# Nine rows in partitions 0-63 and seven in 64-127 for the last head's store of a query-key product

## The chip, the core and the metric

The kernel runs on one core of one Trainium2 chip. The metric is device time in microseconds (us) for one execution; lower is better. Before the change it is 1062.44 us, the median of three runs (1062.24 to 1063.06). The core has five engines that run side by side: PE (TensorE, matmuls), DVE (VectorE), ACT (ScalarE), POOL (GpSimd) and SP (SyncE, which here issues DMAs). Sixteen DMA engines carry data between the chip's HBM and the on-chip memory SBUF, which has 128 partitions. Matmul results land in PSUM and are copied from there to SBUF.

## The reference

```python
def setup_inputs():
    batch, n_heads, seq, head_dim = 8, 12, 1024, 64
    ...
def reference(q, k):
    return np.einsum('bhid,bhjd->bhij', q, k).astype(np.float32)
```

For each of 8 x 12 = 96 heads, the 1024 x 64 matrix q times the transposed 1024 x 64 matrix k: a 1024 x 1024 float32 result, 4 MB for a head and 402.65 MB in all. The inputs are 50.33 MB.

## The kernel before

**Blocks.** The 96 heads go in blocks of 2, 2, 4, 8 and then five times 16 heads (`sizes`). A block's q and k are loaded, cast to float16 on POOL, and transposed so that the 64 elements of a row lie along partitions: by PE in the first two blocks, in 32x32 squares by DVE (L229) in the others. Two heads share the 128 partitions of a transposed tile: the first half of a block's heads in partitions 0-63, the second in 64-127. So the last head of all is in partitions 64-127 of its block's `qT` and `kT`.

**One head** is the work of `scores`. Its 1024 rows are dealt over 128 partitions, eight rows each: row i of the head is on partition i // 8, as its row t = i % 8. For each t, one weight load of 64x128 (L308: every eighth column of `qT`) and two matmuls of 512 columns (L311) fill 128x1024 of PSUM. From the second head on two values of t go together (`w` = 2): four matmuls fill half of PSUM, 128x2048 float32, and one ACT copy (L288) takes it to the output buffer. PSUM has two such regions (`halves_ps`), so PE fills one while ACT empties the other. A head takes four copies.

**Output.** Each head has one of three output buffers `o_sb` of 128 x 8 x 1024 float32, taken in turn (`outs`). When the last of the four copies is done, SP issues one DMA for the whole head (L301): partition p sends its eight rows, 32 KB, to 32 KB of HBM in one piece. The first copy of a head waits until the store that left from the same buffer, three heads ago, has landed (`out_free`, counted by `store_landing`, 16 for each DMA). All 96 stores are on SP's queue, in the order of the heads. At the very end SP waits for all three counts.

**Input buffer.** `x_sb` holds the raw rows of the coming block (q, then k). `input_busy` is the last cast that reads it. After the casts of the last block nothing reads or writes it.

**The helper `multiply`** gives the matmul's tile size as (64, 128) at L320: 64 rows of weights, 128 columns.

Of the kernel before, what the change touches and what calls it, by code (L numbers as in the profile page):

```python
# [8 lines left out]
P = 128  # L9
# [50 lines left out]
def kernel(  # L60
# [6 lines left out]
    nc = tc.nc  # L67

    B, H, S, D = q.shape
    NT = S // P  # L70
# [4 lines left out]
    of = out.rearrange("b h i j -> (b h) i j")  # L75
# [13 lines left out]
    x_sb = pool.tile([P, NMAX * S * D // P], F32, name="x_sb", tag="x")  # L89
# [10 lines left out]
    pe = Engine(nc, nc.tensor, "pe_done")  # L100
    act = Engine(nc, nc.scalar, "act_done")
    dve = Engine(nc, nc.vector, "dve_done")
    gps = Engine(nc, nc.gpsimd, "pool_done")
    sp = Engine(nc, nc.sync, "sp_done")
# [18 lines left out]
    n, at = S * D // P * 2, 8 * S // 2  # L123
# [8 lines left out]
    input_busy = []  # L132
    outs = Ring(o_sb)
    input_landing = [Landing(nc, f"x{i}_in") for i in range(2)]
    store_landing = {id(t): Landing(nc, f"out{i}_out") for i, t in enumerate(o_sb)}

    class Block:
# [117 lines left out]
        def scores(self, n, side, regions, w):  # L255
            half, g = divmod(n, self.N // 2)
            cs = slice(half * D, (half + 1) * D)
            qT = self.qk[0].rearrange("c (g m t) -> c g t m", t=NT, m=P)
            kT = self.qk[1].rearrange("c (g j) -> c g j", j=S)
            buf, out_free, out_busy = outs.next()  # L260
            written = {}
            for u in range(NT // w):
                ps, ps_free, ps_busy = regions.next()
                first = True
                for tt in range(w):
                    stationary = qT[cs, g, w * u + tt]
                    done = pe.run(
                        lambda: load_weights(stationary, half * D),
                        self.ready if n == 0 and u == 0 else [],
                        signal=False,  # L270
                    )
                    for j in range(2):
                        at = tt * S + j * 512
                        done = pe.run(
                            lambda: multiply(
                                ps[:, at : at + 512],
                                stationary,
                                kT[cs, g, j * 512 : (j + 1) * 512],
                                half * D,
                            ),  # L280
                            ps_free,
                            signal=tt == w - 1 and j == 1,
                        )
                dst = buf[:, w * u : w * u + w].rearrange("p t j -> p (t j)")
                by_dve = w == 1 and u % 2
                copier = dve if by_dve else act
                copied = copier.run(
                    lambda: (nc.vector.tensor_copy if by_dve else nc.scalar.copy)(  # L288
                        out=dst, in_=ps[:, : w * S]
                    ),  # L290
                    out_free + [done],
                )
                written[copier] = copied
                ps_busy.append(copied)
                for do in side.get(u, []):
                    do()
            self.over = [done]
            sp.wait(written.values())
            if self.first + n == 0:
                sp.wait(blocks[EARLY].landed[0])  # L300
            dma = nc.sync.dma_start(  # L301
                out=of[self.first + n].rearrange("(p t) j -> p (t j)", p=P),
                in_=buf.rearrange("p t j -> p (t j)"),
            )
            out_busy.append(store_landing[id(buf)].start(dma))

    def load_weights(stationary, at):
        return nc.tensor.ldweights(stationary, tile_position=(at, 0))  # L308

    def multiply(dst, stationary, moving, at):  # L310
        return nc.tensor.add_instruction(  # L311
            mybir.InstMatmult(
                name=nc.get_next_instruction_name(),
                ins=[nc.tensor.lower_ap(moving), nc.tensor.lower_ap(stationary)],
                outs=[nc.tensor.lower_ap(dst)],
                start_tensor_calc=True,
                stop_tensor_calc=True,
                ldweights=False,
                tile_position=(at, 0),
                tile_size=(D, P),  # L320
            )
        )

    blocks, first = [], 0
# [4 lines left out]
    early, _, early_busy = outs.next()  # L329
    raw = early.rearrange("p t j -> p (t j)")  # L330
    at = 0
# [17 lines left out]
    def next_load(eng):  # L349
        if stream:  # L350
            b, x = stream.pop(0)
            earlier = (b.i, 0) if x else (b.i - 1, 1)
            assert b.i == EARLY or not any((i, c[0]) == earlier for i, c in casts)
            b.load(x, eng)

    for x in range(2):
# [7 lines left out]
                out=ident,  # L364
                in_=ident,
# [9 lines left out]
    def to_half(last):  # L375
        while casts:
            i, c = casts[0]
            if i > last or (blocks[i], c[0]) in stream:
                return
            if not (rooms if i == PE_BLOCKS else halves).free():  # L380
                return
            done = blocks[i].cast_quads(*c)
            if i == 2:
                early_busy[:] = [done]
            casts.pop(0)

    def transposed(b, s):
        b.transpose_quads(*s)
        to_half(b.i)

    def block(i, heads, regions, w):
        b = blocks[i]
        nxt = blocks[i + 1] if i + 1 < len(blocks) else None
        for n in heads:
            side = {}
            if nxt and nxt.by_pe:
                if n == 1:
                    side = {
                        u: [
                            lambda x=u // 2: nxt.transpose_rows(  # L400
                                x, regions.next(), dve, nc.vector.tensor_copy
                            )
                        ]
                        for u in (1, 3)
                    }
            elif nxt:
                parts = nxt.chunks()
                at = TURNS if i > EARLY else [m * b.N // len(parts) for m in range(len(parts))]
                some = [s for m, s in zip(at, parts) if m == n]
                side = {0: [lambda s=s: transposed(nxt, s) for s in some]}  # L410
            at = LOADS.get(i, {1: 1, 7: 1})
            if n in at:
                side[at[n]] = side.get(at[n], []) + [lambda: next_load(act)]
            b.scores(n, side, regions, w)
            to_half(i + 2 + (n == b.N - 1))

    for b in blocks[:PE_BLOCKS]:
# [6 lines left out]
    for x in range(2):  # L424
        blocks[0].transpose_rows(
            x, quarters.next(), (dve, act)[x], (nc.vector.tensor_copy, nc.scalar.copy)[x]
        )
        to_half(2)
    block(0, [0], quarters, 1)
    halves_ps = Ring([ps_all[:, 2 * S :], ps_all[:, : 2 * S]])  # L430
    halves_ps.busy = [quarters.busy[2] + quarters.busy[3], quarters.busy[0] + quarters.busy[1]]
    block(0, [1], halves_ps, 2)
    for i in range(1, len(blocks)):
        block(i, range(blocks[i].N), halves_ps, 2)
# [31 lines left out]
```

## Time and profile before

| | |
|---|---|
| time, median of 3 runs (range) | 1062.44 us (1062.24 to 1063.06) |
| time of the profiled execution | 1062.84 us |
| its span, from first to last instruction | 1061.0 us |
| PE busy | 700.2 us (66%) |
| ACT busy | 697.1 us (66%) |
| DVE busy | 431.0 us (41%) |
| POOL busy | 354.2 us (33%) |
| moved by DMA over the span | 453.21 MB, mean 427 GB/s |
| share of the chain that ended last: DMA, ACT, PE | 65%, 16%, 7% |
| one store: size, count, median from issue to landing | 4096 KB, 96, 21.8 us |
| ACT copy of 128x2048 (L288), mean | 1859 ns, 384 in the group |
| matmul of 512 columns (L311), mean | 617 ns, 1536 |

How to read it: the page shows one profiled execution. Its slices cut the span in 40 equal parts and give the busy share of each in tenths; the row for DMA is the mean over the 16 DMA engines. A DMA queue's packet is one piece of a transfer on one engine. The chain that ended last goes back from the last instruction, at each step to what released it. The windows view gives, for stretches of the span in us, each engine's busy time with its instruction count, the clock granted to TensorE, the share of the 16 DMA engines' time taken by the packets that start in the stretch, and GB/s. The granted clock is 1.00 in this kernel.

### The profile page before, as it was taken

To read this page: it belongs to the slowest core of one execution; us is meant where nothing else is said; L and a number is where in the kernel's file an instruction comes from. 1 tells how busy PE (TensorE), PEld (TensorE's weight loads), DVE (VectorE), ACT (ScalarE), POOL (GpSimd) and SP (SyncE) were. 2 spreads that over 40 slices of the span, in tenths; PEclk is the share of its full clock that TensorE was granted. 3 is DMA by queue.
4 is the path that set the end of the run, shared out by engine and by line. 5 is a ranking of instruction groups with operands and counts; after the bars stand their busy time and mean duration, and the time that the engine had idled before them with its cause. 6 is when DMAs were issued, how large, how long until landed. Compare 5 with 4: busy or idle time off the path is not lost.

```text
span 1061.0 us, 3307 instructions
## 1 busy us (share of the span) xinstructions
PE 700.2 (66%) x1568; PEld 127.3 (12%) x800; DVE 431.0 (41%) x55; ACT 697.1 (66%) x386; POOL 354.2 (33%) x206
## 2 busy tenths in 40 slices
PE   6876744957477748567765856775584777778770
PEld 1111100111011101011111101111110111111110
DVE  2995939029193009339003907600761920000000
ACT  4766655857477747567756756775675777777771
POOL 7927465056380028064006509100913700000000
DMA  9999999999999999999999999999999999999997
GB/s 376 434 435 435 434 434 434 416 421 432 431 434 434 435 429 428 426 435 432 432 422 434 435 427 433 433 434 423 433 429 432 435 434 431 434 434 431 432 431 322
DMA packets 17009, 453.21 MB, mean 427 GB/s; under 512 B 1888, under 2 KB 1888, under 8 KB 2912
## 3 DMA queue, kind: packets, MB, share of 16 engines
q1 hardware_dynamic: 14976, 410.00, 89.7%
q10 hardware_dynamic: 2016, 42.99, 9.8%
q8 instruction: 9, 0.15, 0.0%
q14 instruction: 8, 0.07, 0.0%
HBM read 50.33 MB, written 402.65 MB: 427 GB/s over the span
## 4 chain that ended last, share of the span: by engine, by line
DMA 65%; ACT 16%; PE 7%; DVE 5%; POOL 4%; issue 1%; ACTq 0%; SPq 0%
DMA out_dram<-o_sb 60%; ACT o_sb L288 16%; PE ps_all L311 7%; DVE kT L229 4%; POOL half L210 3%; DMA x_sb<-in_k_dram 2%; DMA x_sb<-in_q_dram 2%; DVE qT L229 1%; DMA o_sb<-in_q_dram 0%; PE ps_all L243 0%; POOL qT L181 0%; DVE kT L250 0%; ACT kT L250 0%; ACTq L36 0%; SPq L169 0%
## 5 line engine op out<-in xcount | busy, mean ns | idle before, releaser
L288 ACT COPY o_sb<-ps_all 128x2048 f32<-128x2048 f32 (+1 forms) x384 | 694.8, 1859 | 333.5 <-DMA out_dram<-o_sb 290.2
L311 PE MATMUL ps_all<-kT,qT 64*128 64x512 f16 x1536 | 696.1, 617 | 328.6 <-ACT o_sb L288 312.8
L210 POOL CAST half<-x_sb 32x2048 f16<-32x2048 f32 x176 | 332.3, 1888 | 482.1 <-DMA x_sb<-in_q_dram 302.2
L229 DVE STREAM_TRANSPOSE qT<-half 128x2048 f16<-128x2048 f16 x22 | 202.6, 9478 | 268.1 <-POOL half L210 268.1
L229 DVE STREAM_TRANSPOSE kT<-half 128x2048 f16<-128x2048 f16 x22 | 202.5, 9539 | 137.5 <-POOL half L210 137.5
L308 PEld LDWEIGHTS <-qT 64*128 64x128 f16 x768 | 124.2, 162 | 897.4 <-issue 878.0
L229 DVE STREAM_TRANSPOSE kT<-kT 128x1024 f16<-128x1024 f16 x2 | 9.4, 4870 | 0.0
L229 DVE STREAM_TRANSPOSE qT<-qT 128x1024 f16<-128x1024 f16 x2 | 9.2, 4780 | 0.0
L210 POOL CAST qT<-o_sb 32x1024 f16<-32x1024 f32 x8 | 8.3, 1035 | 1.2 <-DMA o_sb<-in_q_dram 0.8
L210 POOL CAST kT<-o_sb 32x1024 f16<-32x1024 f32 x8 | 8.3, 1035 | 0.5
L250 DVE COPY qT<-ps_all 128x1024 f16<-128x1024 f16 x2 | 2.4, 1224 | 11.1 <-PE ps_all L243 11.1
L288 DVE COPY o_sb<-ps_all 128x1024 f32<-128x1024 f32 x4 | 4.9, 1225 | 4.4 <-PE ps_all L311 4.4
L243 PE MATMUL ps_all<-ident,qT 128*128 128x128 f16 x16 | 2.1, 311 | 6.8 <-POOL qT L181 6.7
L250 ACT COPY kT<-ps_all 128x1024 f16<-128x1024 f16 x1 | 1.0, 1012 | 4.8 <-PE ps_all L243 4.8
L181 POOL CAST qT<-o_sb 128x512 f16<-128x512 f32 x4 | 2.3, 615 | 3.7 <-DMA o_sb<-in_q_dram 3.7
L250 ACT ACT_TABLE_LOAD x1 | 1.3, 1283 | 2.8 <-issue 2.8
L250 DVE COPY kT<-ps_all 128x1024 f16<-128x1024 f16 x1 | 1.2, 1225 | 4.4 <-PE ps_all L243 4.4
L243 PE MATMUL ps_all<-ident,kT 128*128 128x128 f16 x16 | 2.0, 305 | 0.7 <-ACT o_sb L288 0.7
L181 POOL CAST kT<-o_sb 128x512 f16<-128x512 f32 x4 | 2.4, 618 | 0.3 <-DMA o_sb<-in_q_dram 0.3
L243 PEld LDWEIGHTS ps_all<-ident,qT 128*128 128x128 f16 x16 | 1.5, 141 | 7.1 <-POOL qT L181 7.1
L243 PEld LDWEIGHTS ps_all<-ident,kT 128*128 128x128 f16 x16 | 1.5, 136 | 3.3 <-POOL qT L210 1.6
L359 POOL MEMSET ident<- 128x128 f16 x1 | 0.2, 205 | 0.5 <-SPq L98 0.5
(5 smaller groups left out, 0.7 us busy)
## 6 DMA issues: line engine op xcount, KB each, us to landing
out_dram<-o_sb SPq DMA_DIRECT2D x96, 4096.0 KB, 21.8
x_sb<-in_q_dram ACTq DMA_DIRECT2D x5, 4096.0 KB, 24.1
x_sb<-in_k_dram ACTq DMA_DIRECT2D x5, 4096.0 KB, 24.3
x_sb<-in_q_dram SPq DMA_DIRECT2D x1, 2048.0 KB, 14.6
x_sb<-in_k_dram SPq DMA_DIRECT2D x1, 2048.0 KB, 19.5
o_sb<-in_k_dram ACTq DMA_DIRECT2D x4, 256.0 KB, 4.8
o_sb<-in_q_dram SPq DMA_DIRECT2D x4, 256.0 KB, 5.1
o_sb<-in_q_dram SPq DMA_DIRECT2D x1, 1024.0 KB, 8.2
```

Source lines behind the costliest of these rows:

```text
L181: lambda: nc.gpsimd.tensor_copy(out=rows[:, :, h], in_=self.raw[x][:, h * n : (h + 1) * n].rearrange("p (r d) -> p r d", d=D),),
L210: lambda: nc.gpsimd.tensor_copy(out=dst[q0 : q0 + 32].rearrange("p (r d) -> p r d", d=32), in_=raw[32 * b : 32 * b + 32, c * m : (c + 1) * ...
L229: lambda: nc.vector.transpose(out=dst, in_=buf.rearrange("p (r i) -> p r i", i=32)),
L243: lambda: nc.tensor.transpose(t_ps[:, t], rows[:, t], ident),
L250: lambda: copy(out=dst, in_=t_ps.rearrange("c t m -> c m t")), [done]
L288: lambda: (nc.vector.tensor_copy if by_dve else nc.scalar.copy)(out=dst, in_=ps[:, : w * S]),
L308: return nc.tensor.ldweights(stationary, tile_position=(at, 0))
L311: return nc.tensor.add_instruction(mybir.InstMatmult(name=nc.get_next_instruction_name(), ins=[nc.tensor.lower_ap(moving), nc.tensor.lower ...
L359: cleared = gps.run(lambda: nc.gpsimd.memset(ident, 0.0))
```

## The change

The last head of the last block goes through a new function, `scores_uneven`, instead of `scores`; the other 95 heads stay. Rows 0 to 895 of that head are dealt seven to a partition over 128 partitions, rows 896 to 1023 two to a partition over partitions 0-63. So partitions 0-63 hold nine rows and 64-127 seven. The seven are in the output buffer, the extra two in the first 8 KB of `x_sb`. The copies are five: t = 0-1, 2-3, 4-5, 6 alone (128x1024), and the two extra rows (64x2048). After the fourth, SP issues the main store: 128 partitions with 28 KB each. After the fifth it issues eight DMAs of eight partitions with 8 KB each: first partitions 0, 4, ..., 28, then 1, 5, ..., 29, and so on to 3, 7, ..., 31, then the same for 32 to 63. All nine count on the buffer's landing. `multiply` takes the second number of the tile size from the weights' width, 128 everywhere but for the extra rows, where it is 64. An unused `first = True` is dropped.

```diff
+        def scores_uneven(self, n, regions, w):
+            half, g = divmod(n, self.N // 2)
+            cs = slice(half * D, (half + 1) * D)
+            qT = self.qk[0][cs, g * S : (g + 1) * S]
+            kT = self.qk[1][cs, g * S : (g + 1) * S]
+            low, main, extra = P // 2, NT - 1, 2
+            even = qT[:, : P * main].rearrange("c (m t) -> c t m", t=main)
+            more = qT[:, P * main :].rearrange("c (m t) -> c t m", t=extra)
+            buf, out_free, out_busy = outs.next()
+            more_sb = x_sb[:low, : extra * S]
+            rows = [(even[:, t], P, buf[:, t]) for t in range(main)]
+            rows += [(more[:, t], low, more_sb[:, t * S : (t + 1) * S]) for t in range(extra)]
+            groups = [rows[i : i + w] for i in range(0, main - 1, w)]
+            groups += [rows[main - 1 : main], rows[main:]]
+            order = out_free
+            for group in groups:
+                ps, ps_free, ps_busy = regions.next()
+                m = group[0][1]
+                for tt, (stationary, _, _) in enumerate(group):
+                    pe.run(lambda: load_weights(stationary, half * D), signal=False)
+                    for j in range(2):
+                        at = tt * S + j * 512
+                        done = pe.run(
...
+                copied = act.run(
+                    lambda: nc.scalar.copy(out=dst, in_=ps[:m, : k * S]),
+                    order + input_busy + [done],
+                )
+                ps_busy.append(copied)
+                if group is groups[-2]:
+                    sp.wait([copied])
+                    self.store_part(
+                        out_busy,
+                        buf,
+                        of[self.first + n][: P * main].rearrange("(p t) j -> p (t j)", p=P),
+                        buf[:, :main].rearrange("p t j -> p (t j)"),
+                    )
+            self.over = [done]
+            sp.wait([copied])
+            dst = of[self.first + n][P * main :].rearrange("(p t) j -> p (t j)", t=extra)
+            for c in range(0, low, 32):
+                for i in range(4):
+                    self.store_part(
+                        out_busy, buf, dst[c + i : c + 32 : 4], more_sb[c + i : c + 32 : 4]
+                    )
+
+        def store_part(self, out_busy, buf, dst, src):
+            dma = nc.sync.dma_start(out=dst, in_=src)
+            out_busy.append(store_landing[id(buf)].start(dma))
...
-                tile_size=(D, P),
+                tile_size=(D, stationary.shape[1]),
...
-            b.scores(n, side, regions, w)
+            if i == len(blocks) - 1 and n == b.N - 1:
+                b.scores_uneven(n, regions, w)
+            else:
+                b.scores(n, side, regions, w)
```

More of the change, by code (lines that the diff above doesn't have):

```diff
@@ L263, in scores @@
                 ps, ps_free, ps_busy = regions.next()
-                first = True
                 for tt in range(w):
@@ L305, in scores @@
             out_busy.append(store_landing[id(buf)].start(dma))
+        def scores_uneven(self, n, regions, w):
[21 more added lines that the diff above has]
+                        done = pe.run(
+                            lambda: multiply(
+                                ps[:m, at : at + 512],
+                                stationary,
+                                kT[:, j * 512 : (j + 1) * 512],
+                                half * D,
+                            ),
+                            ps_free,
+                            signal=tt == len(group) - 1 and j == 1,
+                        )
+                k = len(group)
+                if m == P:
+                    t = rows.index(group[0])
+                    dst = buf[:, t : t + k].rearrange("p t j -> p (t j)")
+                else:
+                    dst = more_sb
+                copied = act.run(
[18 more added lines that the diff above has]
+                        out_busy, buf, dst[c + i : c + 32 : 4], more_sb[c + i : c + 32 : 4]
+                    )
@@ L413, in block @@
                 side[at[n]] = side.get(at[n], []) + [lambda: next_load(act)]
-            b.scores(n, side, regions, w)
+            if i == len(blocks) - 1 and n == b.N - 1:
+                b.scores_uneven(n, regions, w)
+            else:
+                b.scores(n, side, regions, w)
             to_half(i + 2 + (n == b.N - 1))
```

## The prediction

> **What bounds the kernel now.** I read four views in turn: the page's slices and queues, the chain that ended last, the order of instructions at the end, and the busy windows of the last ten microseconds. The page first:
>
> ```profile
> span 1061.0 us, 3307 instructions
> ...
> DMA  9999999999999999999999999999999999999997
> GB/s 376 434 435 435 434 434 434 416 421 432 431 434 434 435 429 428 426 435 432 432 422 434 435 427 433 433 434 423 433 429 432 435 434 431 434 434 431 432 431 322
> ...
> q1 hardware_dynamic: 14976, 410.00, 89.7%
> q10 hardware_dynamic: 2016, 42.99, 9.8%
> q8 instruction: 9, 0.15, 0.0%
> q14 instruction: 8, 0.07, 0.0%
> ```
>
> The 16 DMA engines are full in 39 of 40 slices, at about 433 GB/s. Only the last slice drops, to 322 GB/s. Two small queues load instructions: nine packets of 16 KB and eight of 8 KB. Every store is 128 packets of 32 KB (4096 KB, one packet per partition), so eight packets per engine. The chain for the last head and its store's issue:
>
> ```profile
> 1008.95 21.72 DMA out_dram<-o_sb
> ...
> 1032.66 1.88 PE ps_all L311 x4
> 1034.53 0.02 issue
> 1034.55 3.63 ACT o_sb L288 x2
> ```
>
> ```profile
> 1038.21 0.33 SPq L301 DMA_DIRECT2D out_dram<-o_sb  x1
> ```
>
> The last head's eight rows are copied by 1034.55 + 3.63 = 1038.18, and SP issues its store at 1038.21. That is early: a store lands 21.72 us after its issue, with two others ahead of it. Eight packets take an engine 9.7 us (below), so 12 of the 21.7 are standing in line. Nothing that PE, ACT or SP does within some 5 us moves the end. What does is when the last of the 16 engines finishes:
>
> ```profile
> core 0: us, PE busy (x) PEld busy (x) DVE busy (x) ACT busy (x) POOL busy (x), PEclk, DMA share, GB/s
> 1051.72:1052.93 1.21, 0.00 (x0) 0.00 (x0) 0.00 (x0) 0.00 (x0) 0.00 (x0) 1.00 1.00 433
> 1052.93:1054.14 1.21, 0.00 (x0) 0.00 (x0) 0.00 (x0) 0.00 (x0) 0.00 (x0) 1.00 0.57 244
> 1054.14:1055.36 1.22, 0.00 (x0) 0.00 (x0) 0.00 (x0) 0.00 (x0) 0.00 (x0) 1.00 0.13 54
> 1055.36:1056.57 1.21, 0.00 (x0) 0.00 (x0) 0.00 (x0) 0.00 (x0) 0.00 (x0) 1.00 0.06 27
> 1056.57:1057.78 1.21, 0.00 (x0) 0.00 (x0) 0.00 (x0) 0.00 (x0) 0.00 (x0) 1.00 0.06 27
> 1057.78:1059.00 1.22, 0.00 (x0) 0.00 (x0) 0.00 (x0) 0.00 (x0) 0.00 (x0) 1.00 0.06 27
> ```
>
> ```profile
> 1055.30:1055.40 0.10, 0.00 (x0) 0.00 (x0) 0.00 (x0) 0.00 (x0) 0.00 (x0) 1.00 0.76 328
> 1058.00:1058.10 0.10, 0.00 (x0) 0.00 (x0) 0.00 (x0) 0.00 (x0) 0.00 (x0) 1.00 0.76 328
> ```
>
> A window counts the packets that start in it, and the windows are as wide as one 32 KB packet lasts (the packet records have 1213 ns). So share times 16 is the number of engines that still start a packet: 16, then 9, 2, 1, 1, 1. Seven engines begin their last packet before 1052.93, seven more before 1054.14, the second last at 1055.34. One alone begins its last three at 1055.65, 1056.86 and 1058.07. It ends at 1058.07 + 1.21 = 1059.28; the span ends 1.75 us later, which I take as fixed. The middle of the pack ends near 1054.2, so the late engine is 5 us behind and the second 2.4 us (1056.55). That fits the instruction queues, if each sits on one engine: a 16 KB load packet lasts 0.615 us in the records and an 8 KB one 0.309, so 9 x 0.615 = 5.5 us and 8 x 0.309 = 2.5 us.
>
> **The change, part by part.**
>
> *Main store, seven rows.* Packets of 28 KB, which the trace doesn't have. The records give 84 ns for 2 KB, 309 for 8, 615 for 16, 1213 for 32: straight enough to read 615 + 12 x 37.4 = 1063 ns. Eight of them: 8.50 us instead of 9.70. An engine with only these is done 1.20 us sooner. Bounds: 0 (a fixed cost per packet, against the row of 84 ns) and 1.21 (pure bytes). I take 1.20.
>
> *Extra rows.* 64 partitions x 8 KB, in eight DMAs, the partitions of each four apart. If each puts one packet on each of eight engines, such an engine gets 8 x 0.309 = 2.47 us and eight end marks of 9 ns (0.07): 8.50 + 2.47 + 0.07 = 11.04 against 9.70, 1.34 us later. A store to half of the engines has no row. Its floor is these 1.34 us; its ceiling is each DMA waiting for the one before, at the 4.8 us that the 256 KB loads took from issue to landing (the nearest row): 8 x 4.8 = 38 us after about 1052, or some 30 us late. I take the floor, because four of those loads went out within 1.82 us and landed in 4.8 to 5.1 us, so they overlapped.
>
> *Which engines.* No view of the trace says which engine carries which partition. The forecast takes it that partitions 0-63 and 64-127 are on different engines, eight each, that the eight-partition DMAs use the eight of the low half, and that the late engine is in the upper half. The Trainium skill, "DMA: Bandwidth & Descriptors", section "The descriptor swizzle", gives engines 0 to 7 the partitions 0 to 63, four neighbours at a time; its section on the semaphore increment of 16 puts an eight-partition DMA on the lowest eight. No run here shows either.
>
> *Issue and compute.* Three copies of two rows, one of one row, then the extra copy of two rows on 64 partitions. From 1034.55 the third ends at 1036.4; the single row is 1.01 us (the 128x1024 copies of the first head), 1037.4, so the main store goes out 0.8 us earlier than now: nothing, it stands in line. The extra matmuls start when the third copy frees the region, 1.88 us to 1038.3; the copy adds 1.86 (1859 ns mean row, 128 partitions; I take the same for 64): 1040.2. SP then issues eight DMAs where the first four loads took 1.82 us, so 0.46 each: 3.6 us, 1043.9. The first engines need them after their main part: they begin the last store near 1054.2 - 9.7 = 1044.5 and are through 28 KB packets at 1053.0. Cover 9 us; behind SP only its final wait. If that cover went, the end would move by what is missing. PE and ACT have nothing after it. The earlier heads keep their instructions on every queue.
>
> *Sum.* Late engine in the upper half: 1059.28 - 1.20 = 1058.08. The second engine, should it be in the low half, ends at 1056.55 + 1.34 = 1057.89, just before; the pack at 1055.5. Profiled execution 1062.84 - 1.20 = 1061.64; it lies 0.40 above the median of the runs, so median 1062.44 - 1.20 = 1061.24.
>
> **Rivals.**
>
> *R1, late engine in the low half.* It gets the 1.34 us more: packets of 8 KB stand behind the 28 KB ones of the one engine that is already last, and the time is 1062.44 + 1.34 = 1063.8, slower than before. For: one of 16 engines loads the 16 KB instruction packets, and no view names it. Against: nothing in the trace. It decides as soon as the late engine holds low partitions.
>
> The Trainium skill, same page, section "Latency and other measured facts", says that engines 7 and 15 are usually slower. By it there would be one late engine in each half, as the trace has just two (5 and 2.4 us behind). If the one 5 us behind is in the upper half, the ends are 1058.08 and 1057.89 and the gain stays 1.20; if not, R1 holds with 1063.8. The rule doesn't choose between the two.
>
> *R2, it doesn't do what it says.* Packets are dealt to engines without regard to partition, or the small DMAs go over all 16 engines. Then each engine has 256 KB as before: four of the 64 packets of 8 KB, 1.24 us, cancel the 1.20. Time 1062.4 to 1062.5. For: the page shows all 16 equally full. Against: every store is cut in eight packets per engine, a fixed deal.
>
> The Trainium skill, same page, "Rules for kernel authors", has it that two transfers to disjoint partition halves both spray over all 16 engines; by it R2 holds for a DMA of 64 partitions, but the change uses DMAs of eight. No run here shows it.
>
> *R3, the small DMAs crowd fewer engines.* All 64 extra packets on one engine: 64 x 0.309 = 19.8 us after its main part, 1053.0 + 19.8 + 1.75 = 1074.6 span, against 1061.0: 1076 us. For: nothing but the lack of a row.
>
> **How the numbers follow.** Forecast 0.52, R1 0.30, R2 0.12, R3 and other serial costs 0.04, the remaining 0.02 a gain beyond the forecast. The trace gives evens between the halves for the late engine; that I put the upper one ahead is a choice, not a reading, and it moves the time by 2.5 us at most. Predicted: 1061.2. The three runs before spread over 0.8 us, so the likeliest case alone is 1060.6 to 1061.8. The range takes in R2 and R1: 1060.5 to 1063.9.
>
> A measurement of this kernel tells about 0.2% (2.1 us) from no change. Forecast, R2 and R1 all lie within it (-1.2, 0, +1.3). With the spread of the runs, 0.05 of the forecast and the 0.02 fall below, 0.05 of R1 and the 0.04 of R3 above: faster 0.07, within 0.84, slower 0.09.
>
> **What would show it.** In the profile after, windows of one packet at the end: if right, the 64 packets of 8 KB lie on eight engines other than the late one, whose last packet starts near 1057.0 and lasts 1.06; the span shrinks by 1.2. R1 shows a string of 8 KB packets at the very end, to 1060.6; R2 the same late engine at the same time. The issue is right if all eight small DMAs leave SP before 1045. Wrong altogether: an 8 KB store packet over 0.4 us, a gap between packets of one engine, or a 28 KB packet that isn't near 1.06 us.

## The result and the profile after

The changed kernel takes 1063.87 us (median of 17 runs, 1063.13 to 1066.33), against 1062.74 us for the kernel before on the same chips (17 runs, 1061.91 to 1064.69). The medians differ by 1.1 us; the ratio is 1.0014, interval 1.0008 to 1.0020, or 0.85 to 2.1 us slower. The prediction named 1061.2 as likeliest, 1.2 us faster. The time lies in its range, beside the rival R1 (1063.8).

The page of the changed kernel, its span, packets and queues:

```profile
span 1061.8 us, 3319 instructions
...
DMA packets 17137, 453.21 MB, mean 427 GB/s; under 512 B 1952, under 2 KB 1952, under 8 KB 2976
...
q1 hardware_dynamic: 15104, 410.00, 89.7%
q10 hardware_dynamic: 2016, 42.99, 9.7%
q8 instruction: 9, 0.15, 0.0%
```

The bytes are the same, with 128 more packets (17137 against 17009): 64 of 8 KB and 64 more end marks (the 4-byte packet with which an engine counts its part of a DMA as landed). The order of SP's and ACT's work for the last head, start and duration in us:

```profile
1036.77 0.33 SPq L367 DMA_DIRECT2D out_dram<-o_sb  x1
1037.78 1.86 ACT L345 COPY x_sb<-ps_all 64x2048 f32<-64x2048 f32 x1 [1.04 <-PE ps_all L374]
1039.67 10.64 SPq L367 DMA_DIRECT2D out_dram<-x_sb  x8
```

The main store is issued 1.4 us earlier than before (0.6 of it because the store that the last head waits for landed earlier, at 1030.09 instead of 1030.66), and the eight small DMAs follow from 1039.67 on. They take SP 1.33 us each (10.64 / 8), not the 0.46 of the prediction, and the last is out at 1050.3. The windows of the end (the five compute engines do nothing there; the last two columns count, the DMA share and GB/s):

```profile
core 0: us, PE busy (x) PEld busy (x) DVE busy (x) ACT busy (x) POOL busy (x), PEclk, DMA share, GB/s
1052.93:1054.14 1.21, 0.00 (x0) 0.00 (x0) 0.00 (x0) 0.00 (x0) 0.00 (x0) 1.00 0.55 230
1054.14:1055.36 1.22, 0.00 (x0) 0.00 (x0) 0.00 (x0) 0.00 (x0) 0.00 (x0) 1.00 0.43 178
1055.36:1056.48 1.12, 0.00 (x0) 0.00 (x0) 0.00 (x0) 0.00 (x0) 0.00 (x0) 1.00 0.17 70
1056.48:1057.50 1.02, 0.00 (x0) 0.00 (x0) 0.00 (x0) 0.00 (x0) 0.00 (x0) 1.00 0.07 28
1057.50:1060.06 2.56, 0.00 (x0) 0.00 (x0) 0.00 (x0) 0.00 (x0) 0.00 (x0) 1.00 0.06 26
1060.06:1061.80 1.74, 0.00 (x0) 0.00 (x0) 0.00 (x0) 0.00 (x0) 0.00 (x0) 1.00 0.00 0
```

```profile
1056.50:1056.60 0.10, 0.00 (x0) 0.00 (x0) 0.00 (x0) 0.00 (x0) 0.00 (x0) 1.00 0.67 287
1057.50:1057.60 0.10, 0.00 (x0) 0.00 (x0) 0.00 (x0) 0.00 (x0) 0.00 (x0) 1.00 0.20 82
1059.70:1059.80 0.10, 0.00 (x0) 0.00 (x0) 0.00 (x0) 0.00 (x0) 0.00 (x0) 1.00 0.20 82
```

From 1056.48 on one engine of 16 works alone (share 0.06). A single packet that starts in a 0.10 us window shows its size: 287 GB/s x 0.10 us is 28 KB at 1056.5, 82 x 0.10 is 8 KB at 1057.5 and at 1059.7. Between 1057.50 and 1060.06, 26 GB/s x 2.56 us is 66 KB, eight packets of 8 KB. So the late engine finishes its 28 KB packets near 1057.58 and then carries a full share of the extra rows. It ends at 1060.07; before, it was 1059.28. This is R1's picture.

### The profile page after: what moved, and what is told of

Same layout as the page of the kernel before. It is cut to its first block, busy times and chain, and to the rows that moved or that the text cites. A ratio compares the mean times of both kernels' runs of the same rounds, so it can differ in the third digit from the quotient of the medians.

```text
span 1061.8 us, 3319 instructions
## 1 busy us (share of the span) xinstructions
PE 701.5 (66%) x1570; PEld 127.4 (12%) x801; DVE 430.9 (41%) x55; ACT 698.1 (66%) x387; POOL 354.4 (33%) x206
## 2 busy tenths in 40 slices
DMA packets 17137, 453.21 MB, mean 427 GB/s; under 512 B 1952, under 2 KB 1952, under 8 KB 2976
## 4 chain that ended last, share of the span: by engine, by line
DMA 65%; ACT 16%; PE 7%; DVE 5%; POOL 4%; issue 1%; ACTq 0%; SPq 0%
DMA out_dram<-o_sb 60%; ACT o_sb L287 15%; PE ps_all L374 7%; DVE kT L229 4%; POOL half L210 3%; DMA x_sb<-in_k_dram 2%; DMA x_sb<-in_q_dram 2%; DVE qT L229 1%; DMA o_sb<-in_q_dram 0%; ACT o_sb L345 0%; PE ps_all L243 0%; ACT x_sb L345 0%; POOL qT L181 0%; DVE kT L250 0%; ACT kT L250 0%
## 5 line engine op out<-in xcount | busy, mean ns | idle before, releaser
L371 PEld LDWEIGHTS <-qT 64*128 64x128 f16 (+1 forms) x769 | 124.4, 162 | 898.9 <-issue 880.8
```

## The experiments

All times are medians, beside the kernel before in the same set of runs. "Packet records" are the start, length and size of every DMA packet in a trace; a packet's record starts 3 or 4 ns before the one ahead of it on the same engine ends, so that an engine's string of packets can be followed. Theory A came out of the trace of the changed kernel: a DMA of few partitions is dealt to the lowest engines, and the late engine is one of the low eight.

**e1_count: which engine is late.** Into the kernel before, behind the last store:

```diff
+    probe = Landing(nc, "probe")
+    sp.wait(input_busy)
+    for m in range(1, 17):
+        dma = nc.sync.dma_start(
+            out=x_sb[:m, (m - 1) * 512 : m * 512],
+            in_=flat[0][: m * 8].rearrange("(p r) d -> p (r d)", p=m),
+        )
+        landed = probe.start(dma)
...
```

> The kernel before, and behind its last store fifteen small loads on SP's queue, of 2, 3, 4 ... 16 partitions with 2 KB each (and one of a single partition), to a part of the input buffer that nothing reads. Theory A: a DMA of m partitions, m up to 16, uses the m lowest engines, one packet each, and the engines take their packets in the order of issue. Then engine n (0 to 15) ends with 16 - n packets of 2 KB behind its eight of 32 KB, and the late engine's count names it: 9 to 16 for an engine of the low eight, 1 to 8 for the high. From the result of the change it must be 9 or more. Rival: small DMAs start on an engine in turn, or by partition; then counts are equal within one or two, or don't fall with the engine. Time: 16 x 0.093 = up to 1.5 us longer at the end.

One run took 1065.43 us, 2.8 over before where up to 1.5 was expected. In its trace the late engine ends 1.3 us later than before; the rest lies behind the last packet and isn't explained. The windows around the late engine's last packets, and the rest of the span:

```profile
1058.30:1058.40 0.10, 0.00 (x0) 0.00 (x0) 0.00 (x0) 0.00 (x0) 0.00 (x0) 1.00 0.77 328
1059.50:1060.59 1.09, 0.00 (x0) 0.00 (x0) 0.00 (x0) 0.00 (x0) 0.00 (x0) 1.00 0.06 23
```

The last 32 KB packet of all starts in 1058.30 to 1058.40 and lasts 1.24 us in the packet records. Behind it, 23 GB/s x 1.09 us is 25 KB, which is twelve packets of 2 KB. The page has 272 more packets on q1 than before: 1 + 2 + ... + 16 = 136 of 2 KB and as many end marks, so a DMA of m partitions ran on m engines. By theory A the late engine, in 12 of the 16 small DMAs, is in those of five partitions and more: number 4, counted from 0 at the bottom. It is in the low eight, and DMAs of four partitions shouldn't reach it (e5_four to e8_own bear that out).

**e2_mirror8: partitions or their number.** In the changed kernel:

```diff
-            more_sb = x_sb[:low, : extra * S]
+            more_sb = x_sb[low:, : extra * S]
```

> The changed kernel with the extra rows on partitions 64-127 instead of 0-63, still in eight DMAs of eight partitions, four apart. Theory A (the number of partitions in the DMA picks the engines, the lowest eight, whichever partitions they are): the late engine still ends with eight packets of 8 KB, and the time is that of the change, about 1.1 us over before. Rival (a partition has its engine): the extra rows leave the late engine, it ends with its eight 28 KB packets, and the time is 1.2 us under before.

1064.44 against 1062.64 us, ratio 1.0016 (1.0008 to 1.0025). The late engine's end:

```profile
1057.30:1057.40 0.10, 0.00 (x0) 0.00 (x0) 0.00 (x0) 0.00 (x0) 0.00 (x0) 1.00 0.67 287
1058.35:1060.88 2.53, 0.00 (x0) 0.00 (x0) 0.00 (x0) 0.00 (x0) 0.00 (x0) 1.00 0.06 26
```

A last packet of 28 KB and then 26 x 2.53 = 66 KB again, though the rows now lie in partitions 64-127. For DMAs of eight the deal goes by the number of partitions, not by which they are. The rival falls: exchanging the halves in the code doesn't mend the change.

**e3_onedma: one DMA of 64 partitions.**

```diff
-            for c in range(0, low, 32):
-                for i in range(4):
-                    self.store_part(
-                        out_busy, buf, dst[c + i : c + 32 : 4], more_sb[c + i : c + 32 : 4]
-                    )
+            self.store_part(out_busy, buf, dst, more_sb)
```

> The changed kernel with the extra rows in one DMA of 64 partitions instead of eight of eight. Theory A: it goes over all 16 engines, four packets of 8 KB each, so that the late engine ends with 8 x 1.063 + 4 x 0.309 = 9.74 us for the last head against 9.70: the time of before within 0.3 us. Rival (a partition has its engine, low half only): as the change, 1.1 us over before.

1063.17 against 1062.64 us, ratio 1.0008 (0.9999 to 1.0016): not clear of noise.

```profile
1058.40:1059.64 1.24, 0.00 (x0) 0.00 (x0) 0.00 (x0) 0.00 (x0) 0.00 (x0) 1.00 0.06 26
```

26 x 1.24 = 32 KB, four packets of 8 KB on the late engine: a sixteenth of the extra rows. It is the deal that R2 described, and R2's time within the interval. The trace ends 0.36 us later than before although the count of bytes is the same: the late engine's last packet of 28 KB took 1.73 us instead of 1.06.

**e4_loads2: why one engine is late.** In the kernel before:

```diff
     def load_weights(stationary, at):
+        nc.tensor.ldweights(stationary, tile_position=(at, 0))
         return nc.tensor.ldweights(stationary, tile_position=(at, 0))
```

> The kernel before with every weight load of the scores issued twice: 768 more PE instructions, and nothing else moved by DMA. Theory B (the late engine is late because it alone loads PE's instructions, 16 KB at a time): some three more packets on the instruction queue of 16 KB, the late engine ends 1.8 to 4 us later and with it the kernel, the second engine and the pack stay. Rival (the late engine is slow by itself, or through something that the instructions don't touch): its lag over the pack stays within 0.5 us, and so does the time.

1064.63 against 1062.64 us, ratio 1.0016 (1.0007 to 1.0025). The page's queue and the windows of the end:

```profile
q8 instruction: 12, 0.20, 0.1%
```

```profile
1054.24:1055.45 1.21, 0.00 (x0) 0.00 (x0) 0.00 (x0) 0.00 (x0) 0.00 (x0) 1.00 0.38 163
1055.45:1056.66 1.21, 0.00 (x0) 0.00 (x0) 0.00 (x0) 0.00 (x0) 0.00 (x0) 1.00 0.25 108
1056.66:1057.87 1.21, 0.00 (x0) 0.00 (x0) 0.00 (x0) 0.00 (x0) 0.00 (x0) 1.00 0.06 27
1057.87:1059.08 1.21, 0.00 (x0) 0.00 (x0) 0.00 (x0) 0.00 (x0) 0.00 (x0) 1.00 0.06 27
1059.08:1060.29 1.21, 0.00 (x0) 0.00 (x0) 0.00 (x0) 0.00 (x0) 0.00 (x0) 1.00 0.06 27
```

Three more packets of 16 KB, 12 for 9. One engine again ends alone, at 1060.85 in the packet records, 1.6 us later than before; the time is 2.0 us over. More PE instructions do make this kernel longer, and the rival (within 0.5 us) falls. But the pack didn't stay: four engines still start a packet after 1055.45, where it was one after 1055.36.

Theory B falls as well, by the packet records. Two windows of the kernel before, in each of which one packet starts:

```profile
978.97:979.00 0.03, 0.03 (x1) 0.00 (x0) 0.00 (x0) 0.03 (x1) 0.00 (x0) 1.00 2.02 546
979.92:979.95 0.03, 0.03 (x1) 0.00 (x0) 0.00 (x0) 0.00 (x0) 0.00 (x0) 1.00 3.30 1092
```

The first is the last of the nine instruction packets: 546 GB/s x 0.03 us is 16 KB, and a share of 2.02 x 16 engines x 0.03 us is 0.97 us. The second is the 32 KB packet that stands behind it on its engine (it starts 14 ns before the first ends), with 3.30 x 16 x 0.03 = 1.58 us. That engine's string of packets ends at 1056.55: it is the second engine, not the late one. In e4_loads2 those at 838.18, 917.93 and 996.25 are on three engines that end at 1057.29, 1056.00 and 1056.87, the first and the last of them among the three new ones behind 1055.45. In both runs the late engine has no instruction packet of 16 KB in its last 200 us. Nor is the price 0.615 us: in both runs such a packet takes 0.88 to 0.97, and the 32 KB packet behind it about 1.6 instead of 1.21, some 1.3 us together.

The late engine falls behind in small steps instead. Before, the last of a store's 16 end marks lies 3.8 us behind their median for the store that lands at 845 us, 5.1 for the one at 1031, some 0.07 us more with each store, and still 5.1 at the end, when PE and ACT are done. In e4_loads2 it is 4.4 at 846, 6.0 at 1032 and 6.1 at the end. So of the 1.6 us in this pair of traces 1.0 is the late engine's own lag, and all engines are 0.6 later. What makes its packets a little longer, and whether PE's instructions have to do with it, stays open.

**e5_four and e6_lean: DMAs that don't reach the late engine.** The 128 extra rows lie on 32 partitions, four rows each:

```diff
-            low, main, extra = P // 2, NT - 1, 2
+            low, main, extra = P // 4, NT - 1, 4
...
+            for c in range(0, low, 4):
+                self.store_part(out_busy, buf, dst[c : c + 4], more_sb[c : c + 4])
```

> The changed kernel with the 128 extra rows on 32 partitions, four rows each, in eight DMAs of four partitions with 16 KB each. Theory A (a DMA of m partitions uses the m lowest engines; the late engine had 12 of the 16 counting packets, so it is number 4 from the bottom and no DMA of four reaches it): the late engine ends with its eight 28 KB packets, near 1058.1 us of the span; the four lowest engines get 8 x 0.615 = 4.9 us more behind theirs, ending between 57.2 and 59.1 depending on which of the pack they are. Time 0.2 to 1.2 us under before, 1.3 to 2.3 under the change. Rival (the deal goes by partition or in turn, and the count of 12 was chance): the late engine has some of the 16 KB packets at its end, each 0.615 us, and the time is that of the change or worse.

1065.46 against 1062.78 us, ratio 1.0027 (1.0017 to 1.0038): slower than any other, where a gain was expected. In e6_lean the list of DMAs is `[(4 * i, 4) for i in range(6)] + [(24, 8)]`:

> As the run with DMAs of four partitions, but the last two of them joined to one DMA of eight partitions. Theory A: the late engine ends with exactly one packet of 16 KB, 8.50 + 0.615 = 9.12 us for the last head against 9.70, so near 1058.7; the four lowest get seven packets. Time 0.6 us under before. Rival (as there): no packet, or several, on the late engine.

1064.18 against 1062.78 us, ratio 1.0014 (1.0005 to 1.0023), again on the wrong side. The packet records of e5_four show where the time goes. After its 28 KB packets the late engine has none of 16 KB, as theory A says (in e6_lean it has one, as expected). But the first four of the 32 packets of 16 KB take 1.7 to 2.1 us and three later ones up to 2.3 (in e6_lean 2.6), where 0.61 is the norm, and the late engine's last packet of 28 KB takes 1.63 instead of 1.06 (in e6_lean 2.21). The last of the four lowest engines ended at 1062.74. The windows of e5_four:

```profile
1053.00:1055.00 2.00, 0.00 (x0) 0.00 (x0) 0.00 (x0) 0.00 (x0) 0.00 (x0) 1.00 0.58 184
1055.00:1057.00 2.00, 0.00 (x0) 0.00 (x0) 0.00 (x0) 0.00 (x0) 0.00 (x0) 1.00 0.33 111
1057.00:1059.00 2.00, 0.00 (x0) 0.00 (x0) 0.00 (x0) 0.00 (x0) 0.00 (x0) 1.00 0.34 80
1059.00:1061.00 2.00, 0.00 (x0) 0.00 (x0) 0.00 (x0) 0.00 (x0) 0.00 (x0) 1.00 0.11 41
1061.00:1063.00 2.00, 0.00 (x0) 0.00 (x0) 0.00 (x0) 0.00 (x0) 0.00 (x0) 1.00 0.09 33
```

A share of 1.00 goes with 433 GB/s elsewhere, so 0.34 should carry 147; it carries 80. Engines are busy and move half as much. I had changed two things with one edit: how many partitions a DMA has, and that they are neighbours. Theory C: several engines that read neighbouring partitions at once get in each other's way.

**e7_apart: the same, eight partitions apart.** Against e5_four:

```diff
-            for c in range(0, low, 4):
-                self.store_part(out_busy, buf, dst[c : c + 4], more_sb[c : c + 4])
+            for i in range(8):
+                self.store_part(out_busy, buf, dst[i::8], more_sb[i::8])
```

> The run with DMAs of four partitions again, the four now eight apart (i, i+8, i+16, i+24) instead of neighbours; everything else the same. Theory C (four engines that read four neighbouring partitions at once get in each other's way, which stretched the 16 KB packets from 0.61 to 1.7-2.3 us): the packets behind the late engine's and the pack's own take 0.61 us, up to 0.9 while other engines read the same partitions' neighbours; the four lowest engines end between 58 and 60 and the time is 0 to 1 us under before. Rival (the stretch comes from HBM's side, or from the size): the packets stay at 1.7 to 2.3 us at first and the time at 1065.5.

1062.78 against 1062.62 us, ratio 1.0003 (0.9994 to 1.0012): the stretch is gone, the hoped-for gain of up to 1 us isn't there. The same windows:

```profile
1053.00:1055.00 2.00, 0.00 (x0) 0.00 (x0) 0.00 (x0) 0.00 (x0) 0.00 (x0) 1.00 0.40 156
1055.00:1057.00 2.00, 0.00 (x0) 0.00 (x0) 0.00 (x0) 0.00 (x0) 0.00 (x0) 1.00 0.31 119
1057.00:1059.00 2.00, 0.00 (x0) 0.00 (x0) 0.00 (x0) 0.00 (x0) 0.00 (x0) 1.00 0.13 55
1059.00:1061.00 2.00, 0.00 (x0) 0.00 (x0) 0.00 (x0) 0.00 (x0) 0.00 (x0) 1.00 0.00 0
```

0.13 with 55 GB/s is the full rate and nothing is left after 1059. The loss against before went from 2.7 us to 0.2 for a change of stride alone. Nearly all packets of 16 KB last 0.61 us; four of the 32 still take 0.9 to 1.5, three of them on the engine that ends last, at 1058.98. The rival of the size falls, since the sizes are the same. HBM's side isn't excluded by this run alone: the rows go to the same places, but four pieces sent at once lay side by side there in e5_four and lie 128 KB apart here. The trace of e2_mirror8 speaks for the on-chip side. Its DMAs have the same sizes and destinations as those of the change, which had all 64 packets of 8 KB at 0.31 us; with only the partitions exchanged, 23 of them took longer (up to 0.64), and four packets of 28 KB, on two engines without extra rows, took 2.0 to 2.1.

The Trainium skill, "SBUF — State Buffer", section "Door 1: The DMA port swizzle", gives each group of four neighbouring partitions, with the group 32 further on, one of 16 DMA ports. These runs agree: four neighbours read at once go with packets of up to 2.3 us, and with a stride of eight nearly all are at 0.61; the part on the group 32 further on isn't shown. By it the change's own "four apart" is what kept its packets at 0.31 us. That this isn't the whole of it e2_mirror8 shows, which has the same stride and stretched packets; why in that half and not in the other isn't shown.

**e8_own and e9_seven: the extra rows on partitions 0-15.** Now the extra rows are the head's first 128, on partitions 0-15 with eight rows each, so that each DMA of four takes one partition of each of four groups of four neighbours. Against the changed kernel, the core of e8_own:

```diff
-            low, main, extra = P // 2, NT - 1, 2
+            low, main, extra = P // 8, NT - 1, 8
...
-            for c in range(0, low, 32):
-                for i in range(4):
-                    self.store_part(
-                        out_busy, buf, dst[c + i : c + 32 : 4], more_sb[c + i : c + 32 : 4]
-                    )
+            for i in range(4):
+                self.store_part(out_busy, buf, dst[i::4], more_sb[i::4])
```

> The 128 extra rows are now the head's first 128 rows, on partitions 0-15 with eight rows each, and leave in four DMAs of four partitions, four apart (i, i+4, i+8, i+12), 32 KB each; matmuls of the extra rows make 32 output partitions of which 16 are copied. Theory A with C: nothing stretches; the late engine ends with its 28 KB packets near 1058.1, the four lowest get 4 x 1.213 = 4.85 us behind theirs and end near 58.0 to 58.9. Time 0.4 to 1.2 us under before. Rival (as in the run before): packets of 32 KB stretched over 1.5 us, time over that of before.

1061.86 against 1062.62 us, ratio 0.9990 (0.9981 to 0.9999): 0.8 us faster than before, just clear of noise. Against the change, which didn't run beside it, that is 1.9 us by the differences of the medians (-0.8 and +1.1), 2.5 by the two ratios.

```profile
1052.93:1054.14 1.21, 0.00 (x0) 0.00 (x0) 0.00 (x0) 0.00 (x0) 0.00 (x0) 1.00 0.53 227
1054.14:1055.36 1.22, 0.00 (x0) 0.00 (x0) 0.00 (x0) 0.00 (x0) 0.00 (x0) 1.00 0.36 154
1055.36:1056.57 1.21, 0.00 (x0) 0.00 (x0) 0.00 (x0) 0.00 (x0) 0.00 (x0) 1.00 0.31 132
1056.57:1057.78 1.21, 0.00 (x0) 0.00 (x0) 0.00 (x0) 0.00 (x0) 0.00 (x0) 1.00 0.18 78
1057.78:1059.00 1.22, 0.00 (x0) 0.00 (x0) 0.00 (x0) 0.00 (x0) 0.00 (x0) 1.00 0.00 0
```

The last packets start before 1057.78 and the last end mark is at 1058.32, 1.0 us earlier than in the kernel before. Several engines now share the end: 0.31 is five of them where one was alone. In the packet records four engines carry four packets of 32 KB each, none over 1.22 us, and end between 1057.1 and 1058.33; the late engine has none of these and ends at 1058.03. In e9_seven the eighth row of each partition goes in one DMA of 16 partitions and the four others carry seven:

```diff
+            cut = (extra - 1) * S
+            self.store_part(out_busy, buf, dst[:, cut:], more_sb[:, cut:])
             for i in range(4):
-                self.store_part(out_busy, buf, dst[i::4], more_sb[i::4])
+                self.store_part(out_busy, buf, dst[i::4, :cut], more_sb[i::4, :cut])
```

> As the run with partitions 0-15, but the eighth row of each of them goes in one DMA of 16 partitions (one packet of 4 KB for each of the 16 engines), and the four DMAs of four carry seven rows, 28 KB. Theory A: the late engine 28 KB x 8 and one of 4 KB, ends near 1058.3; the four lowest 4 x 1.063 + 0.16 = 4.4 us behind their main part, near 57.5 to 58.4. Time 0.8 to 1.1 us under before, the best split of these. Rival: as before.

1061.71 against 1062.62 us, ratio 0.9991 (0.9982 to 1.0000). That is no better and no worse than e8_own within the intervals, and as its own reaches 1.0000 it can't be told from the kernel before.

## Why the prediction was wrong, and where it was right

*What bounds the kernel* held: the end is the end of one late DMA engine. PE, ACT and the time of issue didn't matter: the main store left 1.4 us earlier and the kernel ended later. *Why that engine is late* did not hold. "That fits the instruction queues, if each sits on one engine" is a coincidence of sums: the records have 0.88 to 0.97 us for an instruction packet of 16 KB and not 0.615, and the last one is on the second engine, whose lag behind the median of a store's 16 end marks rose from 1.0 to 2.4 us with it (stores landing at 981.87 and 991.63). With it goes R1's "one of 16 engines loads the 16 KB instruction packets"; R1 itself didn't need it.

*The step that failed* is "Which engines": that "the late engine is in the upper half". The text itself called this "a choice, not a reading". e1_count counted: the late engine is number 4, in the low half, so it carried eight packets of 8 KB (2.49 us) more behind its shorter main part. The forecast's -1.20 us so became R1's +1.34, and the measured difference is 1.1 us (0.85 to 2.1 by the interval). The two prices were sound; they were added on the wrong engine. That the time lies in the range at all is due to R1, which the range takes in.

*A second premise* was read too loosely: "partitions 0-63 and 64-127 are on different engines". For the small DMAs it isn't the partition that chooses; e2_mirror8 put the extra rows in the other half and kept the loss. What the prediction took for them, "the eight-partition DMAs use the eight of the low half", was right in that they go to the same eight engines whichever half the rows lie in, and together with a late engine number 4 it settles the sign.

*The terms.* A 28 KB packet was put at 1063 ns; the records have 1062 (up to 1086 on the late engine). 8 KB: 309 and 309. End marks: 9 and 9. The extra string on the late engine was to take 2.47 + 0.07 us; it ran from 1057.58 to 1060.07, 2.49. It began 0.5 us earlier than 1059.28 - 1.20 = 1058.08. The late engine's lag differs by that much between executions: for the store before the last it is 4.4 us here and 5.1 before, and between 4.65 and 5.58 in the traces of the other versions but e4_loads2. The profiled spans (+0.8 us) show less than the medians (+1.1).

*Issue.* 0.46 us for each small DMA, from loads of 128 partitions, was too small by a factor of three: 1.33. The eight were out at 1050.3 instead of 1043.9. The first packet of 8 KB starts at 1051.47, and its engine would need the eighth 2.2 us later, so the cover of 9 us shrank to some 3 and still held.

*Rivals.* R1 is what happened. R2 is what one DMA of 64 partitions does (e3_onedma), which the Trainium skill's rule, "DMA: Bandwidth & Descriptors", "Rules for kernel authors", says of disjoint halves; the trace agrees for 64 partitions, with four packets of 8 KB on the late engine, and not for eight, with eight of them. R3 has nothing for it. The Trainium skill's "DMA: Bandwidth & Descriptors", "Latency and other measured facts", which has engines 7 and 15 as usually the slower ones, isn't borne out here: the last engine has 12 of the 16 counting packets, and the count for number 7 would be 9, for number 15 it would be 1.

*What would have told.* Nothing in the trace of before names the engines. A probe as in e1_count would have, ahead of any design.

## What to carry to other kernels

When a kernel is bound by DMA to its last byte, look at the last microseconds per engine: a share of 1/16 there is one engine working alone, and what it carries extra sets the time. A sum that happens to fit its lag is no cause: follow its packets. To shift load between engines, count first which one is late with small DMAs of 1 to 16 partitions behind the last store. Then choose the number of partitions of a DMA for the engines that it is to use, and the stride between them so that engines don't read neighbours; change one of the two at a time.

## What the runs showed of the hardware

- A DMA of eight partitions costs SP 0.79 us for the first and 1.33 to 1.38 for the next ones; one of four, 0.33 or 0.74 for the first and 1.1 to 1.3 for the next; one of 64, 0.56; one of 128, 0.33.
- A DMA of m partitions (m up to 16) put one packet on each of m engines, and as far as the late engine tells always the same ones: eight of eight partitions, from either half, gave it eight packets, one of eight gave it one, DMAs of four gave it none.
- Packets for 2, 4, 8, 16, 28 and 32 KB last 84, 159, 309, 611, 1062 and 1213 ns when undisturbed, and 16 KB up to 2.3 us in DMAs of four neighbouring partitions.
- Instructions arrive in packets of 16 KB, nine in 1061 us and three more for 768 more PE instructions, on changing DMA engines beside the data. One takes 0.88 to 0.97 us and stretches the 32 KB packet behind it to 1.6, so its engine is some 1.3 us later.
- One DMA engine, number 4, falls some 0.07 us behind with each store while PE and ACT run, without instruction packets of its own in the last 200 us, and ends about 5 us behind the others' median.
